# One inverse-root chain for the memory's norm and the convolution's layer norm, and the SiLU by token tile

## The chip, the cores and the metric

The kernel runs on one core of a Trainium2 chip. The metric is the device time of one execution in microseconds (us), median of three runs. The engines that matter: TensorE (PE in the profile; its weight loads are PEld) multiplies matrices, VectorE (DVE) and ScalarE (ACT) do elementwise work, GpSimd (POOL) and SyncE (SP) issue transfers. Each engine works through its own queue in the order in which the program wrote it.

## The reference

Two blocks of a transformer-like model on 256 tokens of width 1024, in float32: retention, MoBA attention and a squared-ReLU MLP in the first; in the second four mixing branches with gates, cross attention to a memory of 256 tokens, and a gated feed-forward part. The change touches the second block's mixing stage and the memory's norm:

```python
c_a, c_g = jnp.split(c_u + b_glu[l], 2, axis=-1)
yc = _dwconv_causal(c_a * jax.nn.sigmoid(c_g), conv_dw[l]) + conv_dw_b[l]     # 31 taps, 512 channels
yc = jax.nn.silu(_layer_norm(yc, conv_ln_g[l], conv_ln_b[l]))
...
br = jnp.stack([ya, yf, yc, ys], axis=2)
proj = jnp.einsum('bsnc,ncd->bsnd', br, w_branch[l])
gates = jax.nn.sigmoid(h @ w_gate[l] + b_gate[l]).reshape(B, S, N_BRANCH, D)
mixed = jnp.sum(gates * proj, axis=2) @ w_out[l]
...
m = _rms_norm(mem, norm_mem[l])                  # x * rsqrt(mean(x * x) + 1e-6) * g
xk, xv = jnp.split(m @ w_xkv[l], 2, axis=-1)
```

Both norms need one inverse square root per token, of a variance for the convolution and of a mean square for the memory.

## The kernel before

Every float32 matrix product is made of three matmuls of rounded parts (`mm3`, L254 to L256): a value is split into a high part, written by ScalarE (`whi`, `brh`, `mth`: L174, L250), and a low part, the difference, written by VectorE (`wlo`, `brl`, `mtl`: L180, L251). Weights come in by SyncE's transfers in chunks of 128x1024 (`raw`), are split so, and used once.

The mixing stage goes through `MIX_STEPS`: eight gate groups (1024 input columns, so two chunks of twelve 128x512 matmuls for each of two token tiles, into `ps_as`) and eight branch groups (twelve matmuls for each token tile, into `ps_br`), first gates 0 and 1, then branch j and gate j+2 in turn up to branch 5, with gates 6 and 7 last and branches 6 and 7 behind them. Branches 6 and 7 are the convolution's (`brh[2]`, `brl[2]`); they are the only consumers of the convolution. All of these outputs, and those of the transposes, go through one pool of four PSUM banks (`bank`), taken in rotation: a group of matmuls can start only when VectorE or ScalarE has read what stood in its bank four allocations earlier. A gate tile is read by VectorE (L1299, the bias), a branch tile by L1316 or by L1318 and L1319 (the gate, then the sum into `part`). When both halves of a `part` are complete, four transposes (`ps_mx`) and a split make the input of the output projection `mix`.

Everything beside the matmuls is threaded between them by `tick`, which runs once behind each group of twelve matmuls: it prepares one or two chunks of weights (two only if no lane is alive and three or more chunks wait), takes one step of every lane (a generator in `lanes` or `light`), then some taps of the convolution from `slow` (L956, VectorE, one 128x256 operation each), then the low parts of the weights. How many taps depends on the same count of lanes: up to three without a lane, otherwise no more than `state["taps"]`.

Three of the lanes matter here. `conv_lane` starts behind branch 4, waits until the taps are done and runs `conv_norm`: transposes `ps_ct` (token tiles to partitions), layer-norm statistics, the inverse root by `rstd` (eleven small VectorE operations on 128x2: a first guess by integer arithmetic and three refinements), `cxn` (L974), two empty steps, transposes back (`ps_ct2`, shown as `ps_ct` in the profile), eight SiLU on ScalarE and the split into `brh`, `brl`. `mem_norm` starts behind branch 3: four squares with row sums on ScalarE (`sqm`, `memss`), an add and its own `rstd` on VectorE, four scalings (L1355), and four groups of four transposes (`pt`, `to_T`) with their splits `mth`, `mtl`, which cross attention reads after the mixing stage. The third is each gate's sigmoid, by `later`.

Of the kernel before, what the change touches and what calls it, by code (L numbers as in the profile page):

```python
# [11 lines left out]
F32 = mybir.dt.float32  # L12
# [87 lines left out]
def tile_model(ctx: ExitStack, tc: tile.TileContext, order, wall, x, mem, gains, gain0, pparam, rparam, w_fg,  # L100
# [17 lines left out]
    def stat(name, w=8, dt=F32):  # L118
        return sp.tile([128, w], dt, tag="st", name=name, bufs=16)
# [202 lines left out]
    def tok(t):  # L322
        return slice(t * 128, t * 128 + 128)
# [636 lines left out]
    def conv_norm():  # L960
        ba, pts = stat("ba", 4), []
# [9 lines left out]
        r = rstd(ba[:, 1:4:2], 2, 1.0, "ln")  # L971
# [4 lines left out]
        yield  # L976
        yield
# [7 lines left out]
        for t in range(2):  # L985
            split(brh[2][:, :, tok(t)], brl[2][:, :, tok(t)], tiles(xns[t]))
# [11 lines left out]

    def conv_lane():
        while slow:  # L1000
            yield
        yield from conv_norm()

# [331 lines left out]

    mth, mtl, memn = {}, {}, []

    def mem_load():
        memn.extend(b4([128, D], f"mem{t}") for t in range(2))
        for t in range(2):  # L1340
            nc.gpsimd.dma_start(memn[t], mem[0, tok(t), :])
        return gain("norm_mem_2")

    def mem_norm(gm):
        ss = stat("memss", 4)
        for t in range(2):
            for n in range(2):
                nc.scalar.activation(t2("sqm"), memn[t][:, HS[n]], AF.Square, accum_out=ss[:, 2 * n + t:2 * n + t + 1])
            yield
        nc.vector.tensor_tensor(ss[:, 0:2], ss[:, 0:2], ss[:, 2:4], op=ALU.add)  # L1350
        r = rstd(ss[:, 0:2], 2, 1.0 / D, "mem")
        yield
        for t in range(2):
            for n in range(2):
                nc.vector.scalar_tensor_tensor(memn[t][:, HS[n]], memn[t][:, HS[n]], r[:, t:t + 1], gm[:, HS[n]],  # L1355
                                               op0=ALU.mult, op1=ALU.mult)
            yield
        yield
        for q in range(2):
            mth[q] = b4([128, 4, 256], f"mth{q}", F32R)  # L1360
            mtl[q] = b4([128, 4, 256], f"mtl{q}", F32R)
        for t in range(2):
            for q in range(2):
                to_T(memn[t], t, mth, mtl, (q,))
                yield

    for kind, j in MIX_STEPS:
# [4 lines left out]
        else:  # L1372
# [6 lines left out]
            if j == 0:  # L1379
                gm = mem_load()  # L1380
            if j == 3:
                ml = lane(mem_norm(gm))
    drain(ml)
# [335 lines left out]
```

## Time and profile before

| | us |
|---|---|
| median of three runs | 1256.43 |
| lowest and highest of the three | 1253.81, 1257.52 |
| profiled execution, own time | 1254.88 |
| its span in the trace | 1253.0 |
| TensorE busy | 1236.9 (99%) |
| VectorE busy | 887.8 (71%) |
| ScalarE busy | 674.0 (54%) |

Times in the trace are counted from the start of the span. The stage that the change touches lies between about 915 and 990. A row's time is that of one instruction from start to end; on TensorE the ends of pipelined matmuls overlap the next start, so that there the distance between two starts is what one costs.

### The profile page before, as it was taken

To read this page: it belongs to the slowest core of one execution; us is meant where nothing else is said; L and a number is where in the kernel's file an instruction comes from. 1 tells how busy PE (TensorE), PEld (TensorE's weight loads), DVE (VectorE), ACT (ScalarE), POOL (GpSimd) and SP (SyncE) were. 2 spreads that over 40 slices of the span, in tenths; PEclk is the share of its full clock that TensorE was granted. 3 is DMA by queue.
4 is the path that set the end of the run, shared out by engine and by line. 5 is a ranking of instruction groups with operands and counts; after the bars stand their busy time and mean duration, and the time that the engine had idled before them with its cause. 6 is when DMAs were issued, how large, how long until landed. Compare 5 with 4: busy or idle time off the path is not lost.

```text
span 1253.0 us, 19058 instructions
## 1 busy us (share of the span) xinstructions
PE 1236.9 (99%) x7352; PEld 1093.7 (87%) x7352; DVE 887.8 (71%) x1570; ACT 674.0 (54%) x1078; POOL 13.0 (1%) x34
## 2 busy tenths in 40 slices
PE   9999999999999999999999999999989999999997
PEld 7888888899988888899988999998877897899996
DVE  7866678755556867765556677878997777588773
ACT  7545355644444765654454546654446466667552
POOL 0000000000000000000000000000000000000000
PEclk9999999999999999999999999999999999999999
DMA  9664473756564545565564644356654554456530
GB/s 366 247 204 152 144 252 135 248 191 192 179 198 159 186 139 171 185 215 189 187 214 156 220 140 143 119 167 215 207 202 168 177 197 164 170 184 192 181 116 35
DMA packets 64924, 228.94 MB, mean 183 GB/s; under 512 B 8256, under 2 KB 8512, under 8 KB 64832
## 3 DMA queue, kind: packets, MB, share of 16 engines
q1 hardware_dynamic: 61808, 217.22, 52.1%
q0 software_dynamic: 2880, 10.49, 2.5%
q8 instruction: 58, 0.95, 0.3%
q14 instruction: 34, 0.28, 0.1%
q10 hardware_dynamic: 144, 0.00, 0.0%
HBM read 226.64 MB, written 1.05 MB: 182 GB/s over the span
## 4 chain that ended last, share of the span: by engine, by line
PE 93%; DVE 3%; ACT 2%; issue 1%; DMA 0%; SPq 0%; DVEq 0%; ACTq 0%
PE ps_ws L254 11%; PE ps_ws L256 11%; PE ps_ws L255 11%; PE ps_as L254 8%; PE ps_as L256 8%; PE ps_as L255 8%; PE mlp L291 4%; PE mlp L290 4%; PE mlp L294 4%; PE ffn L291 1%; PE ffn L290 1%; PE ffn L294 1%; DVE wlo L180 1%; PE ret L290 1%; PE ret L291 1%; PE ret L294 1%
## 5 line engine op out<-in xcount | busy, mean ns | idle before, releaser
L180 DVE TENSOR_TENSOR wlo<-raw,whi 128x1024 fp32r<-128x1024 f32 x404 | 477.6, 1220 | 61.7 <-ACT whi L174 60.7
L174 ACT ACTIVATE whi<-raw 128x1024 fp32r<-128x1024 f32 x404 | 406.6, 1049 | 81.2 <-DVE wlo L180 16.4
L254 PE MATMUL ps_ws<-xhi,whi 128*128 128x256 f32 x1120 | 318.8, 285 | 0.0
L256 PE MATMUL ps_ws<-xhi,wlo 128*128 128x256 f32 x1120 | 316.9, 283 | 0.0
L255 PE MATMUL ps_ws<-xlo,whi 128*128 128x256 f32 x1120 | 316.8, 283 | 0.0
L254 PEld LDWEIGHTS ps_ws<-xhi,whi 128*128 128x128 f32 x1120 | 214.7, 192 | 3.5 <-issue 2.0
L255 PEld LDWEIGHTS ps_ws<-xlo,whi 128*128 128x128 f32 x1120 | 214.8, 192 | 1.5
L256 PEld LDWEIGHTS ps_ws<-xhi,wlo 128*128 128x128 f32 x1120 | 214.7, 192 | 0.0
L254 PE MATMUL ps_as<-whi,xhi 128*128 128x512 f32 x480 | 193.0, 402 | 2.5 <-DVE gates L1318 2.3
L255 PE MATMUL ps_as<-wlo,xhi 128*128 128x512 f32 x480 | 188.2, 392 | 0.4 <-DVE wlo L180 0.4
L256 PE MATMUL ps_as<-whi,xlo 128*128 128x512 f32 x480 | 188.3, 392 | 0.0
L254 PEld LDWEIGHTS ps_as<-whi,xhi 128*128 128x128 f32 x480 | 90.6, 189 | 20.7 <-ACT whi L174 2.5
L256 PEld LDWEIGHTS ps_as<-whi,xlo 128*128 128x128 f32 x480 | 90.5, 189 | 20.4 <-DVE xlo L636 0.4
L255 PEld LDWEIGHTS ps_as<-wlo,xhi 128*128 128x128 f32 x480 | 90.6, 189 | 19.3 <-DVE wlo L180 0.9
L291 PE MATMUL mlp<-wlo,act 128*128 128x512 f32 x240 | 93.7, 390 | 0.0
L290 PE MATMUL mlp<-whi,act 128*128 128x512 f32 x240 | 93.5, 390 | 0.0
L753 DVE SCALAR_TENSOR_TENSOR relu<-ps_ws,relu 128x512 f32<-128x512 f32 x24 | 16.6, 691 | 87.1 <-ACT relu L752 87.1
L752 ACT ACTIVATE relu<-ps_ws 128x512 f32<-128x512 f32 x24 | 14.4, 598 | 113.8 <-PE ps_ws L256 113.8
L294 PE MATMUL mlp<-whi,act 128*128 128x512 f32 x240 | 74.0, 389 | 0.0
L294 PEld LDWEIGHTS mlp<-whi,act 128*128 128x128 f32 x240 | 45.1, 188 | 9.6
L291 PEld LDWEIGHTS mlp<-wlo,act 128*128 128x128 f32 x240 | 45.2, 188 | 8.6
L290 PEld LDWEIGHTS mlp<-whi,act 128*128 128x128 f32 x240 | 45.2, 188 | 8.5
(434 smaller groups left out, 1580.2 us busy)
## 6 DMA issues: line engine op xcount, KB each, us to landing
raw<-in_wall_dram SPq DMA_DIRECT2D x404, 512.0 KB, 4.3
gate_bias<-in_gains_dram POOLq DMA_DIRECT2D x4, 512.0 KB, 5.9
h<-in_x_dram SPq DMA_DIRECT2D x4, 256.0 KB, 5.1
raw<-in_wall_dram SPq DMA_DIRECT2D x4, 256.0 KB, 4.1
gainln_mix_post<-in_gains_dram POOLq DMA_DIRECT2D x2, 512.0 KB, 6.2
gainln_mlp_pre<-in_gains_dram POOLq DMA_DIRECT2D x2, 512.0 KB, 7.8
gainln_mlp_post<-in_gains_dram POOLq DMA_DIRECT2D x2, 512.0 KB, 6.8
mem<-in_mem_dram POOLq DMA_DIRECT2D x2, 512.0 KB, 6.4
```

The source lines that it names most:

```text
L174: nc.scalar.activation(hi, raw, AF.Copy)
L180: nc.vector.tensor_tensor(lo, raw, hi.bitcast(F32), op=ALU.subtract)
L254: nc.tensor.matmul(o, ah, bh, start=start, stop=False)
L255: nc.tensor.matmul(o, ah, bl, start=False, stop=False)
L256: nc.tensor.matmul(o, al, bh, start=False, stop=stop)
L290: nc.tensor.matmul(acc[t][n], ah[:, k, ts], wh[k][:, ns], start=st, stop=False)
L291: nc.tensor.matmul(acc[t][n], ah[:, k, ts], wl[k][:, ns], start=False, stop=False)
L294: nc.tensor.matmul(acc[t][n], al[:, k, ts], wh[k][:, ns], start=False, stop=False)
L752: nc.scalar.activation(r, ps, AF.Relu)
L753: nc.vector.scalar_tensor_tensor(r, ps, 0.0, r, op0=ALU.max, op1=ALU.mult)
```

## The change

The memory's lane is gone. `mem_load` is as before; the four squares now open `conv_lane` (behind branch 4, with the division by 1024 in their scale), the add of the two row sums writes into two further columns of the layer norm's statistics, and one `rstd` over four columns serves both norms. The two empty steps of `conv_norm` now hold the four scalings, one token tile a step. The transposes and splits of the memory became `mem_T`, a lane that starts when `conv_norm` has ended. In `conv_norm` the SiLU and the split go by token tile: four SiLU, split, four SiLU, split.

```diff
     def conv_norm():
-        ba, pts = stat("ba", 4), []
+        ba, pts = stat("ba", 8), []
...
-        r = rstd(ba[:, 1:4:2], 2, 1.0, "ln")
+        nc.vector.tensor_tensor(ba[:, 5:8:2], mss[:, 0:2], mss[:, 2:4], op=ALU.add)
+        r = rstd(ba[:, 1:8:2], 4, 1.0, "ln")
         xns = [t2("cxn") for _ in range(2)]
...
         yield
-        yield
-        yield
+        for t in range(2):
+            for n in range(2):
+                nc.vector.scalar_tensor_tensor(memn[t][:, HS[n]], memn[t][:, HS[n]], r[:, 2 + t:3 + t], memg[0][:, HS[n]],
+                                               op0=ALU.mult, op1=ALU.mult)
+            yield
         br(2)
...
         for t in range(2):
             for i in range(4):
                 nc.scalar.activation(xns[t][:, tok(i)], pts[t][:, tok(i)], AF.Silu, bias=ppc("ln_b", i), scale=ppc("ln_g", i))
-        for t in range(2):
             split(brh[2][:, :, tok(t)], brl[2][:, :, tok(t)], tiles(xns[t]))
         yield
...
+    def mem_T():
+        for q in range(2):
+            mth[q] = b4([128, 4, 256], f"mth{q}", F32R)
+            mtl[q] = b4([128, 4, 256], f"mtl{q}", F32R)
+        for t in range(2):
+            for q in range(2):
+                to_T(memn[t], t, mth, mtl, (q,))
+                yield
+
     def conv_lane():
+        for t in range(2):
+            for n in range(2):
+                nc.scalar.activation(t2("sqm"), memn[t][:, HS[n]], AF.Square, scale=1.0 / math.sqrt(D),
+                                     accum_out=mss[:, 2 * n + t:2 * n + t + 1])
+            yield
         while slow:
             yield
         yield from conv_norm()
+        memg.append(lane(mem_T()))
...
-    def mem_norm(gm):
...
             if j == 4:
                 cl = lane(conv_lane())
             if j == 0:
-                gm = mem_load()
-            if j == 3:
-                ml = lane(mem_norm(gm))
-    drain(ml)
+                mem_load()
+    drain(memg[1])
```

Two consequences can't be seen in the diff. Between branch 3 and branch 4 no lane is alive any more, so `tick` takes more taps and chunks there, and the taps end one tick earlier; with them `conv_norm` starts one tick earlier. The lines of the program shift too: L1299, L1318, L1319, L1355 and L974 of before are L1328, L1347, L1348, L980 and L976 after.

The first place is VectorE around the end of gate 5 and branch 4. Before (the first row is the last of the memory's inverse root; `yc` are taps, `wlo` weights, `gates<-ps_as` and `gates<-ps_br` the reading of a PSUM bank):

```order
L311 SCALAR_TENSOR_TENSOR z_mem<-a_mem,z_mem 128x2
L956 SCALAR_TENSOR_TENSOR yc<-cu,pp,yc 128x232
L956 SCALAR_TENSOR_TENSOR yc<-cu,pp,yc 128x231
L180 TENSOR_TENSOR wlo<-raw,whi 128x1024
L1299 TENSOR_TENSOR gates<-ps_as,gate_bias 128x512
L1355 SCALAR_TENSOR_TENSOR mem_8569<-mem_8569,z_mem,gainnorm_mem_8573 128x512 x2
L956 SCALAR_TENSOR_TENSOR yc<-cu,pp,yc 128x231
L956 SCALAR_TENSOR_TENSOR yc<-cu,pp,yc 128x230
L180 TENSOR_TENSOR wlo<-raw,whi 128x1024
L1318 TENSOR_TENSOR gates<-ps_br,gates 128x512
L1319 TENSOR_TENSOR part<-part,gates 128x512
L1355 SCALAR_TENSOR_TENSOR mem_8570<-mem_8570,z_mem,gainnorm_mem_8573 128x512 x2
```

And after, at the same place of the program:

```order
L956 SCALAR_TENSOR_TENSOR yc<-cu,pp,yc 128x233 x2
L180 TENSOR_TENSOR wlo<-raw,whi 128x1024
L1328 TENSOR_TENSOR gates<-ps_as,gate_bias 128x512
L956 SCALAR_TENSOR_TENSOR yc<-cu,pp,yc 128x232 x2
L956 SCALAR_TENSOR_TENSOR yc<-cu,pp,yc 128x231 x2
L956 SCALAR_TENSOR_TENSOR yc<-cu,pp,yc 128x230 x2
L180 TENSOR_TENSOR wlo<-raw,whi 128x1024
L1328 TENSOR_TENSOR gates<-ps_as,gate_bias 128x512
L956 SCALAR_TENSOR_TENSOR yc<-cu,pp,yc 128x229 x2
L180 TENSOR_TENSOR wlo<-raw,whi 128x1024 x2
L1347 TENSOR_TENSOR gates<-ps_br,gates 128x512
L1348 TENSOR_TENSOR part<-part,gates 128x512
```

The memory's chain and its four scalings have left, and taps that stood later have come in front of branch 4.

The second place is VectorE from the end of the layer norm's inverse root to branch 6. Before:

```order
L311 SCALAR_TENSOR_TENSOR z_ln<-a_ln,z_ln 128x2
L974 TENSOR_SCALAR cxn<-ps_ct,ba,z_ln 128x512 x2
L180 TENSOR_TENSOR wlo<-raw,whi 128x1024
L1299 TENSOR_TENSOR gates<-ps_as,gate_bias 128x512
L180 TENSOR_TENSOR wlo<-raw,whi 128x1024 x2
L1299 TENSOR_TENSOR gates<-ps_as,gate_bias 128x512
L251 TENSOR_TENSOR brl_9416<-cxn,brh_9415 128x4x128 x2
L180 TENSOR_TENSOR wlo<-raw,whi 128x1024 x2
L1318 TENSOR_TENSOR gates<-ps_br,gates 128x512
L1319 TENSOR_TENSOR part<-part,gates 128x512
```

And after:

```order
L311 SCALAR_TENSOR_TENSOR z_ln<-a_ln,z_ln 128x4
L976 TENSOR_SCALAR cxn<-ps_ct,ba,z_ln 128x512 x2
L180 TENSOR_TENSOR wlo<-raw,whi 128x1024
L980 SCALAR_TENSOR_TENSOR mem_8570<-mem_8570,z_ln,gainnorm_mem_8574 128x512 x2
L180 TENSOR_TENSOR wlo<-raw,whi 128x1024
L1328 TENSOR_TENSOR gates<-ps_as,gate_bias 128x512
L980 SCALAR_TENSOR_TENSOR mem_8571<-mem_8571,z_ln,gainnorm_mem_8574 128x512 x2
L180 TENSOR_TENSOR wlo<-raw,whi 128x1024
L251 TENSOR_TENSOR brl_9345<-cxn,brh_9344 128x4x128 x2
L180 TENSOR_TENSOR wlo<-raw,whi 128x1024
L1328 TENSOR_TENSOR gates<-ps_as,gate_bias 128x512
L180 TENSOR_TENSOR wlo<-raw,whi 128x1024
```

The two pairs of memory scalings now stand between `cxn` and the split `brl` of the convolution, each with a chunk of weights behind it.

The third is TensorE around the transposes of the convolution's normed tiles. Before, at the end of gate 7 and the start of branch 6 (the numbers are those of the tiles):

```order
L254 MATMUL ps_as_9379<-whi_9155,xhi_6474 128x512
L255 MATMUL ps_as_9379<-wlo_9156,xhi_6474 128x512
L256 MATMUL ps_as_9379<-whi_9155,xlo_6476 128x512
L317 MATMUL ps_ct2_9417<-ident_98,cxn_9352 128x128 x4
L317 MATMUL ps_ct2_9418<-ident_98,cxn_9353 128x128 x4
L254 MATMUL ps_br_9449<-whi_9188,brh2_9415 128x512
L255 MATMUL ps_br_9449<-wlo_9189,brh2_9415 128x512
L256 MATMUL ps_br_9449<-whi_9188,brl2_9416 128x512
```

And after, where these are rows from the middle of gate 7's second token tile:

```order
L254 MATMUL ps_as_9328<-whi_9061,xhi_6473 128x512
L255 MATMUL ps_as_9328<-wlo_9062,xhi_6473 128x512
L256 MATMUL ps_as_9328<-whi_9061,xlo_6475 128x512
L317 MATMUL ps_ct2_9346<-ident_98,cxn_9277 128x128 x4
L317 MATMUL ps_ct2_9347<-ident_98,cxn_9278 128x128 x4
L254 MATMUL ps_as_9328<-whi_9087,xhi_6474 128x512
L255 MATMUL ps_as_9328<-wlo_9088,xhi_6474 128x512
L256 MATMUL ps_as_9328<-whi_9087,xlo_6476 128x512
```

The transposes now have the last twelve matmuls of gate 7 behind them and branch 6 only after those. The four groups of transposes of the memory, which stood in branch 5 and gate 6, now stand in branches 6 and 7, one behind each twelve matmuls; on ScalarE the rows `cxn` (SiLU) and `brh` alternate as the diff shows.

## Rows read from the trace of the kernel before

**Rows 1.** Page, busy time and share of the span of each engine.
```profile
PE 1236.9 (99%) x7352; PEld 1093.7 (87%) x7352; DVE 887.8 (71%) x1570; ACT 674.0 (54%) x1078; POOL 13.0 (1%) x34
```

**Rows 2.** What TensorE waited for, whole span: us, times, longest.
```profile
PE ps_br L254 <- ACT brh L250: 3.1, 1, 3.1
PE ps_as L254 <- DVE gates L1318: 2.3, 1, 2.3
```

**Rows 3.** Windows: busy (x) of PE, PEld, DVE, ACT, POOL; clock, DMA share, GB/s.
```profile
920.00:930.00 10.00, 9.91 (x46) 7.87 (x44) 9.90 (x18) 4.79 (x7) 0.00 (x0) 1.00 0.60 193
930.00:940.00 10.00, 6.84 (x26) 5.42 (x27) 9.89 (x16) 3.46 (x5) 0.00 (x0) 0.83 0.43 147
...
960.00:970.00 10.00, 6.92 (x23) 5.08 (x22) 5.59 (x8) 9.45 (x16) 0.00 (x0) 0.83 0.46 159
```

**Rows 4.** PE's timeline at the second place: start, us, instruction, idle before.
```profile
956.44 0.39 PE L254 MATMUL ps_as<-whi,xhi 128*128 128x512 f32 x1
...
959.16 1.03 PE L317 MATMUL ps_ct<-ident,cxn 128*128 128x128 f32 x8
963.27 0.50 PE L254 MATMUL ps_br<-whi,brh 128*128 128x512 f32 x1 [3.08 <-ACT brh L250]
...
964.81 0.59 PE L256 MATMUL ps_br<-whi,brl 128*128 128x512 f32 x1
...
968.18 0.43 PE L255 MATMUL ps_br<-wlo,brh 128*128 128x512 f32 x1
```

**Rows 5.** PE's timeline at the first place.
```profile
929.53 0.39 PE L256 MATMUL ps_br<-whi,brl 128*128 128x512 f32 x1
930.89 0.66 PE L317 MATMUL pt<-ident,mem 128*128 128x128 f32 x4 [0.98 <-DVE gates L1318]
933.82 0.50 PE L254 MATMUL ps_as<-whi,xhi 128*128 128x512 f32 x1 [2.27 <-DVE gates L1318]
934.12 0.62 PE L255 MATMUL ps_as<-wlo,xhi 128*128 128x512 f32 x1
...
937.53 0.40 PE L254 MATMUL ps_as<-whi,xhi 128*128 128x512 f32 x1
```

**Rows 6.** DVE's timeline at the first place.
```profile
918.08 0.15 DVE L1350 TENSOR_TENSOR memss<-memss 128x2 f32<-128x2 f32 x1
...
920.33 0.82 DVE L956 SCALAR_TENSOR_TENSOR yc<-cu,pp,yc 128x232 f32<-128x232 f32 x2
...
922.80 1.40 DVE L1355 SCALAR_TENSOR_TENSOR mem<-mem,z_mem,gainnorm_mem 128x512 f32<-128x512 f32 x2
924.13 0.82 DVE L956 SCALAR_TENSOR_TENSOR yc<-cu,pp,yc 128x231 f32<-128x231 f32 x2
...
932.99 0.68 DVE L1318 TENSOR_TENSOR gates<-ps_br,gates 128x512 f32<-128x512 f32 x1
...
934.31 0.69 DVE L251 TENSOR_TENSOR mtl<-pt,mth 128x512 fp32r<-128x512 f32 x1
```

**Rows 7.** ACT's timeline at the second place.
```profile
958.13 1.28 ACT L984 ACT_TABLE_LOAD   x1
959.80 2.90 ACT L984 ACTIVATE cxn<-ps_ct,pp 128x128 f32<-128x128 f32 x8 [0.39 <-PE ps_ct L317]
962.56 1.18 ACT L250 ACTIVATE brh<-cxn 128x512 fp32r<-128x512 f32 x2
```

**Rows 8.** DVE's timeline ahead of the second place.
```profile
947.58 0.69 DVE L1299 TENSOR_TENSOR gates<-ps_as,gate_bias 128x512 f32<-128x512 f32 x1 [0.62 <-PE ps_as L256]
...
949.32 0.69 DVE L969 BATCH_NORM_STATS2 bs<-ps_ct 128x6 f32<-128x512 f32 x1
...
953.23 1.53 DVE L974 TENSOR_SCALAR cxn<-ps_ct,ba,z_ln 128x512 f32<-128x512 f32 x2
954.68 1.21 DVE L180 TENSOR_TENSOR wlo<-raw,whi 128x1024 fp32r<-128x1024 f32 x1
955.81 0.68 DVE L1299 TENSOR_TENSOR gates<-ps_as,gate_bias 128x512 f32<-128x512 f32 x1
```

More of the change, by code (lines that the diff above doesn't have):

```diff
@@ L997, in tile_model, with mem_load @@
         ws_chunk(("list256", "w_in_2", C_U + i * 128, C_U + 512 + i * 128), evac)
-    def conv_lane():
+    mth, mtl, memn, memg = {}, {}, [], []
+    mss = cp.tile([128, 4], F32, name="memss")
+    def mem_load():
+        memn.extend(b4([128, D], f"mem{t}") for t in range(2))
+        for t in range(2):
+            nc.gpsimd.dma_start(memn[t], mem[0, tok(t), :])
+        memg.append(gain("norm_mem_2"))
+    def mem_T():
[6 more added lines that the diff above has]
+                yield
+    def conv_lane():
+        for t in range(2):
+            for n in range(2):
+                nc.scalar.activation(t2("sqm"), memn[t][:, HS[n]], AF.Square, scale=1.0 / math.sqrt(D),
+                                     accum_out=mss[:, 2 * n + t:2 * n + t + 1])
+            yield
         while slow:
@@ L1333, in mixed @@
             split(a[0][:, :, tok(t)], a[1][:, :, tok(t)], tiles(pt[:, c * 256:c * 256 + 256]))
[L1336 to L1342, printed above, removed]
-    def mem_norm(gm):
[L1345 to L1365, printed above, removed]
     for kind, j in MIX_STEPS:
```

## The prediction

> **What bounds the kernel now.** I read the page's busy times first, then what TensorE waited for, then the ten-microsecond windows of the changed stretch, and last the timelines of TensorE, VectorE and ScalarE there. The busy times [rows 1] name TensorE: 1236.9 of 1253.0 us, with VectorE at 71% and ScalarE at 54%. So an instruction taken off VectorE or ScalarE is worth only the wait of TensorE that it ends. The two longest of those waits [rows 2] stand in the stage that the change touches: 3.1 us for `brh` on ScalarE and 2.3 us for an evacuation on VectorE (L1318). The windows [rows 3] show what else they cost: 930 to 940 and 960 to 970 have TensorE busy for 6.84 and 6.92 us, and the granted clock, 1.00 in the window before, is 0.83 in both.
>
> **The price of the two places.** TensorE's steady pitch is 2.72 us for twelve 128x512 matmuls (956.44 to 959.16 [rows 4]), 0.227 us each.
> First place: the `pt` transposes at 930.89 waited 0.98 us and the first matmul of gate 6, at 933.82, waited 2.27 us [rows 5]: 3.25 us. Then the matmuls run at the lower of the clock's two levels (1.2 GHz): eight from 934.12 to 937.53 take 3.41 us where 1.82 would do, 1.59 lost, and the first pitch (0.30) loses 0.07. Sum 4.91.
> Second place: branch 6 at 963.27 waited 3.08 us [rows 4]; its first five pitches, to 964.81, take 1.54 instead of 1.14 (0.40 lost), the next eight, to 968.18, 3.37 instead of 1.82 (1.55 lost). Sum 5.03.
> Together 9.94 us. This is the most that this stage can give.
>
> **Part 1, VectorE around branch 4.** Before, VectorE stands some 6 us behind TensorE there: the evacuation for which gate 6 waits starts at 932.99 [rows 6] and belongs to the first unit of branch 5, which ended before the second unit's 2.72 us began, and that one's last matmul stands at 929.53 [rows 5], so around 927. What put it behind is in the same rows: the chain of small `memss`/`z_mem` operations from 918.08 to 920.33 (2.25 us for twelve, 0.19 each) and the two pairs of memory scalings (922.80 to 924.13, so 1.33 a pair, 2.66 together). Further on, four `mtl` splits (0.69 at 934.31, of which the next operation overlaps 0.08, as everywhere on this engine: 0.6) stand among the evacuations of branch 5 and gate 6. All of that leaves. In exchange four more taps come ahead of branch 4 (0.82 a pair at 920.33, so 0.74), which is work that stood a little later, not new work. So VectorE reaches the first evacuation of branch 4 about when its matmuls end, and the distance of 6 us shrinks to one or two. The waits of 0.98 and 2.27 us need a lag of more than the three spare banks; I take both, and the slow clock behind them, as gone: -4.91.
> The four groups of transposes that leave this place are not saved, they stand later on TensorE: 0. The four squares on ScalarE, each about as long as a `brh` (1.18 for two [rows 7]), now start a little later in a stretch where ScalarE is idle more than half of the time (4.79 us busy from 920 to 930 [rows 3]): 0.
>
> **Part 2, from the layer norm to branch 6.** The transposes `ps_ct2` now stand ahead of the last twelve matmuls of gate 7, so ScalarE has 2.72 us of TensorE's work as a cover that it did not have. Before, the SiLU started 0.64 us after the transposes (959.16 [rows 4], 959.80 [rows 7]), eight took 2.90 us with the splits right behind at 962.56 (0.35 each to there), and TensorE stood until 963.27. After, counted from the end of gate 6 as zero: TensorE runs gate 7 (48 matmuls, 10.88) with the eight transposes in it (1.03 in their row [rows 4], which the next matmul overlaps by some 0.2, so 0.8), so branch 6 could start at 11.7 and its third matmul, the first that reads `brl`, at 12.15.
> ScalarE: the transposes start at 8.16, SiLU of tile 0 at 8.8, four SiLU end at 10.2, the split at 10.8. `brh` is 0.9 us early. The table load of 1.28 us stands ahead of it with nothing queued before it that is late: hidden, with over a microsecond to spare. Were the cover gone, its 1.28 us would lie on the path.
> VectorE: already before, it waited 0.62 us for the end of this gate tile (947.58 [rows 8]); with less ahead of it, it waits longer. Then it has, in one queue: the evacuation (0.2 until it starts, for a matmul's row ends 0.16 after its pitch; 0.69 less 0.08, 0.60); the statistics and the inverse root, 3.91 (949.32 to 953.23 [rows 8]), plus one small add, 0.19; `cxn` 1.45; weights 1.13 (954.68 to 955.81); memory tile 0, 1.33; weights 1.13; evacuation 0.60; memory tile 1, 1.33; weights 1.13. That is 13.0. The inverse root over four columns instead of two I take at the same price, since 512 columns cost 0.60 us and 2 columns 0.19, so that two more add nothing that shows. Then `brl` of tile 0, the shape of `mtl`, 0.65: ready at 13.65. **TensorE is there at 12.15, so the third matmul of branch 6 waits 1.5 us.** This is a new wait: the memory scalings and a weight split, not the SiLU, now stand ahead of `brl`. Queued behind that matmul is all of TensorE. The bounds are 0 (VectorE 1.5 us ahead of this walk) and the 3.08 of before.
> So of 5.03 us this part returns about 3.5: -3.5.
>
> **Part 3, branches 6 and 7.** The transposes of the memory now stand between their units. A unit of TensorE is 2.72 plus four transposes, some 0.4: 3.1 us. VectorE has per unit two operations of the evacuation (932.99 to 934.31 [rows 6], 1.32), `mtl` 0.6 and weights 1.13: 3.06. They are level, and four banks lie between them. In the last two units a pair of `act` splits comes on top; I expect up to 0.2 us, and take 0. Its upper bound is the first place of before, where the same mixture made TensorE wait 3.25 us.
>
> **Sum.** -4.91 - 3.5 = -8.4 us. Against the profiled execution's own 1254.88 us that is 1246.5; the median of the three runs stands 1.55 us above that execution, so on the median 1256.43 I forecast **1248.0 us**. The runs of before lie 3.7 us apart; 0.3% (3.8 us) is about what a measurement here can tell from no change.
>
> **The rivals.**
> *The clock falls after the new wait.* Both places of before were followed by the lower level, and what 0.98 us does by itself can't be told, because 2.27 us come right behind it. If 1.5 us is enough, 1.6 to 2.0 us come back: 1249.8. The Trainium skill, "TensorE: Matmul & The Clock Gate", section "HAM oscillation — how this bites in real kernels", has a kernel whose every wait between groups of matmuls is followed by a group at half clock; the trace agrees for 2.27 and 3.08 us, and no run here shows 1.5. Chance 0.25.
> *No new wait.* VectorE keeps up and the whole 9.9 us are gained: 1246.5 on the median. Against it: the sum of 13.65 has no large uncertain term. Chance 0.12.
> *The second place is only renamed.* If `brl` or `brh` comes 3 us late after all, only the first place pays, -4.9: 1251.5. For it: some twenty operations of VectorE between gate 6 and `brl` have to follow one another without a hole. Chance 0.09.
> *Nothing moves.* If TensorE's busy rows were not what sets the time, the two waits would be filled elsewhere: 1256.4. The Trainium skill, "Perfetto Trace Analysis", section "Identifying the Most-Contended Engine", holds the busy share of matmuls a poor measure, and wants the share of weight loads read instead; by that 87% [rows 1] would leave 13% open on TensorE. Against the mechanism: while nothing is waited for, the matmuls keep 0.227 us apart, and the share not busy in the two windows is what the two waits add up to. The same end results if new waits of 6 us or more in branches 6 and 7 eat the gain. Chance 0.07.
> *Slower.* One mechanism: VectorE's queue in branches 6 and 7. If each of the four units with memory transposes costs what the first place cost with its clock, 4.91, that is +19.6 - 8.4, or 1267.6. One such unit leaves a gain of 3.5; two make it slower by 1.4; it takes two and a half to be slower by over 0.3%. For it: the same operations did stop TensorE before. Against it: they met VectorE then with 6 us of lag and taps in the queue, and there are no taps left here. Chance 0.04.
>
> **How the numbers follow.** The forecast itself has 0.43. Its own range, from 0.7 us more or less of the new wait and the scatter of the runs, is 1246.5 to 1249.5. Forecast, clock fall, no wait and part of the third rival make 0.8 with 1245.0 to 1251.3. Faster by over 0.3% (below 1252.7): 0.43 + 0.25 + 0.12 + 0.09, less a little for the scatter, 0.88. Within 0.3%: 0.08. Slower: 0.04.
>
> **What would show it.** Right: no wait for L1318 around branch 5, clock 1.00 there; VectorE idle for a microsecond or two before the last evacuation of gate 6; `ps_ct2` followed by twelve gate matmuls; one wait of some 1.5 us at the third matmul of branch 6, put down to `brl`, none to `brh`; no wait above 0.3 us among the memory's transposes. Wrong: a wait on `pt` or `ps_mx` in branches 6 and 7, a wait on `brh`, or a clock below 1.00 around branch 6.

## The result, and the profile after

| | before, us | after, us |
|---|---|---|
| median of four runs | 1256.76 | 1245.97 |
| lowest and highest | 1253.81, 1257.52 | 1245.57, 1246.07 |
| profiled execution, own time | 1254.88 | 1246.03 |
| its span | 1253.0 | 1244.3 |

Of before, a fourth run (1257.09) has joined the three that the forecast started from. The ratio of the means is 0.9918, with a 95% interval of 0.9901 to 0.9935: faster by 0.8%. The forecast was 1248.0 with a range of 1245.0 to 1251.3. Against the profiled executions the sum of the prediction, -8.4 us, meets -8.85; the medians lie 10.8 us apart, for a reason that the last section takes up.

The page's first line, and the list of what TensorE waited for (us in total, times, longest), both of the changed kernel:

```profile
PE 1233.0 (99%) x7352; PEld 1091.8 (88%) x7352; DVE 885.7 (71%) x1559; ACT 674.0 (54%) x1078; POOL 13.0 (1%) x34
```

```profile
PE warm L621 <- POOL ident masks.py:199: 1.4, 1, 1.4
PE ps_br L256 <- DVE brl L251: 1.2, 1, 1.2
```

The two waits of [rows 2] are gone from the list. In their place stands one of 1.2 us, for `brl`. TensorE's busy time fell by 3.9 us with the same 7352 matmuls, about the 3.6 us that the prediction gave the slow clock. The windows of the stage (columns as in [rows 3]) say the same:

```profile
930.00:940.00 10.00, 10.00 (x50) 8.37 (x49) 9.64 (x14) 5.46 (x9) 0.00 (x0) 1.00 0.69 227
...
950.00:960.00 10.00, 8.77 (x44) 7.01 (x43) 9.90 (x14) 9.65 (x17) 0.00 (x0) 1.00 0.63 211
```

Where 930 to 940 had 6.84 us of TensorE at a clock of 0.83 there are now 10.00 at 1.00, and the only window that is not full, 950 to 960, lacks 1.23 us.

The timelines around the second place, first VectorE's:

```profile
930.37 0.69 DVE L1347 TENSOR_TENSOR gates<-ps_br,gates 128x512 f32<-128x512 f32 x1
...
941.65 0.69 DVE L1328 TENSOR_TENSOR gates<-ps_as,gate_bias 128x512 f32<-128x512 f32 x1 [1.94 <-PE ps_as L256]
...
946.23 1.53 DVE L976 TENSOR_SCALAR cxn<-ps_ct,ba,z_ln 128x512 f32<-128x512 f32 x2
...
948.81 1.41 DVE L980 SCALAR_TENSOR_TENSOR mem<-mem,z_ln,gainnorm_mem 128x512 f32<-128x512 f32 x2
...
951.87 1.41 DVE L980 SCALAR_TENSOR_TENSOR mem<-mem,z_ln,gainnorm_mem 128x512 f32<-128x512 f32 x2
...
954.33 1.29 DVE L251 TENSOR_TENSOR brl<-cxn,brh 128x512 fp32r<-128x512 f32 x2
```

then ScalarE's:

```profile
947.12 1.28 ACT L989 ACT_TABLE_LOAD   x1 [2.21 <-DVE cxn L976]
950.25 1.51 ACT L989 ACTIVATE cxn<-ps_ct,pp 128x128 f32<-128x128 f32 x4 [1.85 <-PE ps_ct L317]
951.79 0.63 ACT L250 ACTIVATE brh<-cxn 128x512 fp32r<-128x512 f32 x1
```

then TensorE's:

```profile
949.62 1.03 PE L317 MATMUL ps_ct<-ident,cxn 128*128 128x128 f32 x8
...
953.23 0.39 PE L254 MATMUL ps_br<-whi,brh 128*128 128x512 f32 x1
953.45 0.39 PE L255 MATMUL ps_br<-wlo,brh 128*128 128x512 f32 x1
955.07 0.50 PE L256 MATMUL ps_br<-whi,brl 128*128 128x512 f32 x1 [1.23 <-DVE brl L251]
955.40 0.40 PE L254 MATMUL ps_br<-whi,brh 128*128 128x512 f32 x1
```

Read them against the walk of the prediction. VectorE waits 1.94 us for the end of gate 6 (941.65), and from there it has no hole until `brl` begins at 954.33. `brh` of tile 0 was ready at 952.42 (951.79 and 0.63), 0.8 us before branch 6 could start; TensorE issued that branch's first two matmuls at 953.23 and 953.45, stood 1.23 us, and took the third at 955.07. The next one followed after 0.33 us and from there on all were at the full clock. The memory's transposes, between the units of branches 6 and 7, have no entry in the list of waits.

### The profile page after: what moved, and what is told of

The parts are those of the page before. It is cut to its first block, busy times and chain, and to the rows that moved or that the text cites. A ratio compares the mean times of both kernels' runs of the same rounds, so it can differ in the third digit from the quotient of the medians.

```text
span 1244.3 us, 19056 instructions
## 1 busy us (share of the span) xinstructions
PE 1233.0 (99%) x7352; PEld 1091.8 (88%) x7352; DVE 885.7 (71%) x1559; ACT 674.0 (54%) x1078; POOL 13.0 (1%) x34
## 4 chain that ended last, share of the span: by engine, by line
PE 94%; DVE 3%; ACT 2%; issue 1%; DMA 0%; SPq 0%; DVEq 0%; ACTq 0%
PE ps_ws L254 11%; PE ps_ws L255 11%; PE ps_ws L256 11%; PE ps_as L256 8%; PE ps_as L254 8%; PE ps_as L255 8%; PE mlp L291 4%; PE mlp L290 4%; PE mlp L294 4%; PE ffn L291 1%; PE ffn L290 1%; PE ffn L294 1%; PE ps_br L256 1%; PE ps_br L255 1%; PE ps_br L254 1%; DVE wlo L180 1%
```

## The experiments

All of them ran beside the kernel before; a median is that of four runs unless it says otherwise, and of ten for two of them.

**1. What the SiLU by token tile is worth.** The changed kernel with whole SiLU:

```diff
             for i in range(4):
                 nc.scalar.activation(xns[t][:, tok(i)], pts[t][:, tok(i)], AF.Silu, ...)
+        for t in range(2):
             split(brh[2][:, :, tok(t)], brl[2][:, :, tok(t)], tiles(xns[t]))
```

> The changed kernel, with the eight SiLU first and then both splits, as before. My theory: the SiLU by token tile is not what pays, since the split of tile 0 (brl on VectorE) waits for VectorE's queue and not for ScalarE. In the changed kernel brh of tile 0 was ready at 952.4 and brl began at 954.33; with whole SiLU brh comes some 1.5 us later, 953.9, still ahead of 954.33. TensorE would then wait some 0.7 us for brh (953.23 to 953.9) and 0.8 instead of 1.23 us for brl: the same time as the changed kernel, 1246.0, within 0.5 us. Rival, the SiLU by tile is what ended the second wait: 1.5 us or more come back, 1247.5 to 1249, with the longest wait put down to brh.

Measured 1246.10 us, ratio 0.9923 (0.9906 to 0.9939): the changed kernel's time. Its waits:

```profile
PE ps_br L256 <- DVE brl L251: 0.6, 1, 0.6
...
PE ps_br L254 <- ACT brh L250: 0.3, 1, 0.3
```

The time is the one forecast. The 1.2 us for `brl` split up into 0.3 for `brh` and 0.6 for `brl`, where 0.7 and 0.8 were reckoned: the waits were over-sized, but counted between the starts of the matmuls the two together cost the same 1.4 us as the one wait did. So in the changed kernel this part of the edit is hidden behind VectorE.

**2. The same part alone, on the kernel before.** The reverse of that diff.

> The kernel before with the SiLU and the split by token tile and nothing else. My theory: without a cover the SiLU is on the path there, so parting it pays where it stands: brh of tile 0 comes 1.4 us earlier, the wait at branch 6 falls from 3.08 to 1.7 us, and brl of tile 0 right behind, so that a second wait of 0.2 to 0.3 us comes at the third matmul. Gain 1.1 to 1.4 us, and 2.7 to 3.2 if the clock then stays up: 1253.5 to 1255.3 against 1256.6. Rival, brl or the table load decides and nothing is gained: 1256.6.

Measured 1252.70 us (ten runs, 1251.75 to 1255.43) against 1255.35 of before (nineteen runs), ratio 0.9983 (0.9973 to 0.9993). So without a cover it does pay. How much of the 2.65 us is its own can't be read from the medians, because of the clock: three of the ten runs have a mean granted clock of 0.995, the others 0.998 to 0.999, and in the trace the clock differs already at the first place, ahead of the edit. TensorE's timeline at the first place:

```profile
931.77 0.66 PE L317 MATMUL pt<-ident,mem 128*128 128x128 f32 x4 [0.97 <-DVE gates L1317]
934.68 0.47 PE L254 MATMUL ps_as<-whi,xhi 128*128 128x512 f32 x1 [2.26 <-DVE gates L1317]
934.99 0.39 PE L255 MATMUL ps_as<-wlo,xhi 128*128 128x512 f32 x1
935.22 0.40 PE L256 MATMUL ps_as<-whi,xlo 128*128 128x512 f32 x1
```

This is the wait of [rows 5], 0.97 and 2.26 us, and behind it the matmuls stand 0.23 us apart, not 0.43. At the second place `brh` was waited for 2.29 us, more than the 1.7 that I gave. With no slow matmuls ahead, TensorE was there 0.7 us earlier, and the SiLU could not follow, since it began as soon as its table was loaded (958.29 and 1.28, then 959.58). ScalarE's rows, then TensorE's wait:

```profile
958.29 1.28 ACT L984 ACT_TABLE_LOAD   x1
959.58 1.50 ACT L984 ACTIVATE cxn<-ps_ct,pp 128x128 f32<-128x128 f32 x4
961.12 0.63 ACT L250 ACTIVATE brh<-cxn 128x512 fp32r<-128x512 f32 x1
...
961.80 0.50 PE L254 MATMUL ps_br<-whi,brh 128*128 128x512 f32 x1 [2.29 <-ACT brh L250]
```

**3. What the shared chain is worth.** The changed kernel with a chain of its own for the memory, at the same place:

```diff
-        nc.vector.tensor_tensor(ba[:, 5:8:2], mss[:, 0:2], mss[:, 2:4], op=ALU.add)
-        r = rstd(ba[:, 1:8:2], 4, 1.0, "ln")
+        nc.vector.tensor_tensor(mss[:, 0:2], mss[:, 0:2], mss[:, 2:4], op=ALU.add)
+        rm = rstd(mss[:, 0:2], 2, 1.0, "mem")
+        r = rstd(ba[:, 1:4:2], 2, 1.0, "ln")
...
```

> The changed kernel, with an inverse-root chain of its own for the memory again, at the place of the shared one. My theory: the stretch from gate 6 to brl is VectorE's, so the eleven small operations come on the path with their full time, some 2.1 us: the wait for brl grows from 1.23 to 3.3 us, and the clock falls behind it as it did before (1.6 to 2.0 us more): 1246.0 + 3.7 to 4.1, so 1249.7 to 1250.1. Rival, the chain is hidden (its sum is ready long before, and a wait on something else ends last): 1246.0, no change in the wait. Second rival, the wait grows but the clock stays: 1248.1.

Measured 1250.17 us, ratio 0.9957 (0.9943 to 0.9972): 4.2 above the changed kernel, where 3.7 to 4.1 were forecast. TensorE's timeline:

```profile
954.09 0.47 PE L254 MATMUL ps_br<-whi,brh 128*128 128x512 f32 x1 [0.74 <-ACT cxn L990]
...
957.06 0.73 PE L256 MATMUL ps_br<-whi,brl 128*128 128x512 f32 x1 [2.27 <-DVE brl L251]
957.59 0.63 PE L254 MATMUL ps_br<-whi,brh 128*128 128x512 f32 x1
958.02 0.63 PE L255 MATMUL ps_br<-wlo,brh 128*128 128x512 f32 x1
```

Waits of 0.74 and 2.27 us in place of 1.23, and behind them a pitch of 0.43. The profile puts the 0.74 down to a SiLU of the second token tile, which this unit does not read. VectorE's reading of gate 7's first tile, whose bank the unit takes, ended just then too (953.26 and 0.68 us, where it begins at 951.27 in the changed kernel); which of the two was waited for is not shown. Eleven operations of 0.2 us cost four microseconds at this place, 1.7 of them by the clock (eight pitches from 957.06 to 960.58 take 3.52 us, not 1.82).

**4. The same chain at another place.** The kernel before, with the start of the memory's lane moved and everything else as it was:

```diff
-            if j == 3:
+            if j == 5:
                 ml = lane(mem_norm(gm))
```

> The kernel before, with one line changed: the memory's lane starts behind branch 5 and not behind branch 3. Its chain of its own stays, and the SiLU stays whole. My theory: the place of the memory's work is what pays, not the sharing of the chain. The chain falls where VectorE waits for gate 6 in any case (1.94 us idle in the changed kernel), the taps move as in the changed kernel, the transposes back get their cover, and the scalings stand ahead of brl as there. Expected: first place gone, one wait of 1.2 to 2 us at branch 6, 1246.0 to 1246.8, the time of the changed kernel within 0.8 us. Rival, the sharing is what pays: some 2.2 us of chain come back on the path, 1248.2 or more.

Measured 1249.21 us (1247.83 to 1249.58), ratio 0.9949 (0.9933 to 0.9966): my number was missed by 2.4 to 3.2. The profiled execution is the fastest of the four (1247.83, granted clock 0.999 on the mean of the whole execution); the other three, 1249.15 to 1249.58, have a mean of 0.997, so a stretch at the lower clock fits for them, on top of what the trace shows. What it shows is neither the chain nor `brl`:

```profile
953.59 0.66 PE L317 MATMUL pt<-ident,mem 128*128 128x128 f32 x4 [2.81 <-DVE gates L1299]
```

In this order the first memory transposes stand in gate 7, and their bank is the one of gate 7's first tile, which VectorE reads only behind both memory scalings. So a further empty step ahead of the transposes was put in, which brings them behind gate 7 and between the units:

```diff
             yield
         yield
+        yield
         for q in range(2):
             mth[q] = b4([128, 4, 256], f"mth{q}", F32R)
```

> The kernel before with the memory's lane started behind branch 5 and one more empty step ahead of its transposes, so that these stand behind branch 6's units as in the changed kernel; the chain of its own and the whole SiLU stay. In the run with the lane behind branch 5 alone, the longest wait was 2.8 us of the first memory transposes for a PSUM bank (they had moved into gate 7), and none was left for brh or brl; its own chain ended with VectorE only 0.3 us later at the layer norm than in the changed kernel. My theory: what made that run slower is the bank, not the chain. Expected here: the waits of the run with whole SiLU (0.3 for brh, 0.6 to 0.9 for brl), 1246.0 to 1246.6. Rival, the chain costs its 2.2 us: 1248.0 or more, with a wait of 3 us for brl.

Measured 1248.31 us (1247.61 to 1248.48), ratio 0.9938 (0.9923 to 0.9954). By the number alone the rival, 1248.0 or more, would have it; its wait of 3 us for `brl` is not there (0.6). VectorE's timeline further on, first of the changed kernel and then of this one:

```profile
993.58 0.68 DVE L385 TENSOR_TENSOR y<-mix,gainnorm_mix_post 128x512 f32<-128x512 f32 x1
...
1052.16 1.42 DVE L411 SCALAR_TENSOR_TENSOR h<-y,r,h 128x512 f32<-128x512 f32 x2
```

```profile
993.57 0.68 DVE L385 TENSOR_TENSOR y<-mix,gainnorm_mix_post 128x512 f32<-128x512 f32 x1
...
1052.14 1.42 DVE L411 SCALAR_TENSOR_TENSOR h<-y,r,h 128x512 f32<-128x512 f32 x2
```

At the end of the output projection and again 59 us later the two kernels stand at the same time to 0.02 us. The whole difference between these two executions, 1.6 us (2.3 between the medians), comes behind that, in the first matmuls of the next stage:

```profile
1060.72 0.50 PE L254 MATMUL ps_as<-whi,xhi 128*128 128x512 f32 x1 [0.34 <-ACT whi L174]
1061.98 0.50 PE L255 MATMUL ps_as<-wlo,xhi 128*128 128x512 f32 x1 [0.76 <-DVE wlo L180]
```

These wait for weights (`whi`, `wlo`), which `tick` prepares; that the one tick that this kernel has fewer in the mixing stage makes them late fits (ScalarE has split 51 chunks from 900 to 1055 us and not 52, and is one behind from 980 on), but no run tried it. In the mixing stage itself a chain of its own, put where VectorE waits for gate 6 in any case, costs nothing. Sharing is worth 4 us where the chain stands on the path and, in that stage, nothing where it stands in the hole; why the kernel as a whole is still slower stays open.

**5. What the chain did at the first place.** The kernel before with the memory scaled by its sum of squares, without the inverse root (this part of the norm is left out):

```diff
-        r = rstd(ss[:, 0:2], 2, 1.0 / D, "mem")
+        r = ss
```

> The kernel before without the memory's inverse root (the sum of squares scales the memory instead, so this part of the norm is left out): eleven small operations fewer on VectorE, all else in its place. My theory: the chain is one part of VectorE's lag of 6 us at the first place, so 2.0 us of the waits there end: 0.98 vanishes and 2.27 becomes 1.2 or so, and if the clock then stays up another 1.6 us: second place untouched. Gain 2.0 without, 3.6 with the clock: 1253 to 1254.7 against a median of 1256.6. Rival, the chain alone made the first place: the whole 4.9 us are gained, 1251.7, no wait on L1318 left.

Measured 1252.23 us (ten runs) against 1255.35, ratio 0.9974 (0.9965 to 0.9983). At the first place one wait is left:

```profile
932.99 0.47 PE L254 MATMUL ps_as<-whi,xhi 128*128 128x512 f32 x1 [1.40 <-DVE gates L1318]
```

1.40 us in place of 0.98 and 2.27, so 1.85 us for 2.1 us of VectorE's operations, and the clock stayed up there. The second place did not stay as it was: TensorE was there earlier, the SiLU began only behind its table load (956.59 and 1.28, then 957.88), and the wait for `brh` grew from 3.08 to 3.59 us, with a longer stretch at the lower clock behind it. This profiled execution, 1254.00, is the slowest of the ten. The chain made more than half of the first place's wait; what made the rest, the scalings, the `mtl` splits or their places, no run took apart.

**6. The cover of the SiLU.** The changed kernel with one more step ahead of the transposes back:

```diff
             yield
+        yield
         br(2)
```

> The changed kernel with one more empty step ahead of the transposes back, so that they stand right ahead of branch 6, as before; scalings and SiLU by tile as in the changed kernel. My theory: the twelve gate matmuls behind the transposes are the cover of the SiLU. Without them TensorE stands from the end of the transposes until brh of tile 0 is there: SiLU 0.64 us after the transposes begin, four of them 1.45, split 0.6, that is 2.7 less the 0.8 of the transposes, 1.9 us, and with brl behind it another 0.3 or so: 2.2 to 2.5 us instead of 1.23, and perhaps the lower clock behind it. 1247.0 to 1247.3 without the clock's fall, 1248.6 to 1249.3 with it. Rival, the cover is worth nothing because VectorE's queue decides: 1246.0 within 0.4.

Measured 1250.22 us, ratio 0.9958 (0.9943 to 0.9972). Without the cover the kernel is 4.2 us slower, more than I forecast. ScalarE's timeline has the term that I left out, and the last row is TensorE's wait:

```profile
952.01 0.63 ACT L1330 ACTIVATE gates<-gates 128x512 f32<-128x512 f32 x1 [7.08 <-DVE gates L1329]
...
953.60 1.28 ACT L990 ACT_TABLE_LOAD   x1
954.89 1.50 ACT L990 ACTIVATE cxn<-ps_ct,pp 128x128 f32<-128x128 f32 x4
...
957.11 0.80 PE L254 MATMUL ps_br<-whi,brh 128*128 128x512 f32 x1 [3.71 <-ACT brh L250]
```

The sigmoid of gate 7's first tile (952.01), which in the changed kernel stands behind the SiLU, now stands ahead of it in ScalarE's queue, and had waited 7.08 us for VectorE's evacuation of that tile. Behind it come a chunk of weights and the table load, 1.28 us, and the SiLU starts 0.01 us after that. So the table load was on the path, and TensorE's wait was 3.71 us, not 2.2 to 2.5, with the slow clock behind it (pitches of 0.43). In the changed kernel the same load began at 947.12 and was done 1.85 us before the SiLU could start. The 4.2 us are thus the cover, the order in ScalarE's queue and the clock together.

**7. More work ahead of `brl`.** The changed kernel with two more scalings into a spare tile, read by nobody:

```diff
+        for _ in range(2):
+            nc.vector.scalar_tensor_tensor(t2("dum"), memn[0][:, HS[0]], r[:, 2:3], memg[0][:, HS[0]], op0=ALU.mult, op1=ALU.mult)
         br(2)
```

> The changed kernel with two more 128x512 scalings into a spare tile on VectorE, ahead of brl (1.33 us of work that nothing reads). My theory: brl is set by VectorE's queue, so the wait at the third matmul of branch 6 grows by 1.33, from 1.23 to 2.56 us, and 1.3 us come on the time: 1247.3. As to the clock: before, it fell behind waits of 3.08 and of 0.98 and 2.27 together, and in the changed kernel it stayed at 1.00 behind 1.23. If 2.56 is enough, 1.6 us more: 1248.9. Rival, VectorE's queue has room: 1246.0.

Measured 1249.04 us, ratio 0.9947 (0.9932 to 0.9962).

```profile
956.31 0.80 PE L256 MATMUL ps_br<-whi,brl 128*128 128x512 f32 x1 [2.54 <-DVE brl L251]
956.90 0.63 PE L254 MATMUL ps_br<-whi,brh 128*128 128x512 f32 x1
957.33 0.63 PE L255 MATMUL ps_br<-wlo,brh 128*128 128x512 f32 x1
```

A wait of 2.54 us, 1.31 more than 1.23 for 1.33 us of work, and then the lower clock: both numbers as forecast.

**8. Four ways to take the new wait away.** First, the second memory tile's scaling between the two `brl`:

```diff
-        for t in range(2):
+        def scale_mem(t):
             for n in range(2):
...
-            yield
+        scale_mem(0)
+        yield
+        yield
         br(2)
...
             split(brh[2][:, :, tok(t)], brl[2][:, :, tok(t)], tiles(xns[t]))
+            if t == 0:
+                scale_mem(1)
         yield
```

> The changed kernel, with the scalings of the memory's second token tile between the brl splits of tile 0 and tile 1 and no longer ahead of both. My theory: brl of tile 0 then starts 1.33 us earlier, 953.0, just where TensorE needs it (953.68), and the last new wait ends: 1.2 to 1.5 us less, 1244.6. VectorE's work in branches 6 and 7 is the same in the same order, so nothing is late behind it; a wait of up to 0.5 us on pt or ps_br would show that I am wrong there. Rival, something beside the scalings holds brl (brh on ScalarE, weights): 1246.0 and the wait still there.

Measured 1246.01 us, ratio 0.9923 (0.9908 to 0.9938). The wait for `brl` is gone and the time is the same. Here I was wrong: work behind it was late enough to take the gain back.

```profile
968.30 0.63 PE L317 MATMUL ps_mx<-ident,part 128*128 128x128 f32 x4 [0.46 <-DVE act L251]
```

The last `ps_mx` transposes wait 0.46 us for an `act` split, and with smaller delays ahead of them the first `mix` matmul starts at 968.68, 0.04 us from where it starts in the changed kernel (968.72). That made VectorE's queue as a whole the suspect, and two kernels take the scalings off it. In both, ScalarE multiplies by the inverse root ahead of its table load. The gain is multiplied by GpSimd behind the squares in the one, and by VectorE in its hole of 1.94 us in the other:

```diff
+                nc.gpsimd.tensor_tensor(memn[t][:, HS[n]], memn[t][:, HS[n]], memg[0][:, HS[n]], op=ALU.mult)    # the one
...
+                nc.vector.tensor_tensor(memn[t][:, HS[n]], memn[t][:, HS[n]], memg[0][:, HS[n]], op=ALU.mult)    # the other, ahead of the statistics
...
-                nc.vector.scalar_tensor_tensor(memn[t][:, HS[n]], memn[t][:, HS[n]], r[:, 2 + t:3 + t], memg[0][:, HS[n]], ...)
+                nc.scalar.activation(memn[t][:, HS[n]], memn[t][:, HS[n]], AF.Copy, scale=r[:, 2 + t:3 + t])
```

> The changed kernel with the memory's scaling taken off VectorE: GpSimd multiplies by the gain right behind the squares, and ScalarE by the inverse root ahead of its table load, where it stands idle. When the wait for brl alone was taken away (memory tile 1 between the two brl), the whole gain came back as lateness of the ps_mx splits on VectorE, so that my theory now is: from the end of gate 6 to the first mix matmuls VectorE's queue as a whole is the bound. Without its 2.66 us of scalings brl starts when brh is there (952.4), ahead of TensorE (953.7), and the splits for mix are early too: 1.4 us less than the changed kernel, 1244.6. Rival, another bound stands right behind (ScalarE's SiLU, a bank): 1245.5 to 1246. A GpSimd that slows VectorE's operations while it works would show in their durations around 930.

Measured 1248.98 us, ratio 0.9944 (0.9929 to 0.9960): slower than the changed kernel by 3.0. GpSimd's four multiplications (930.11 to 937.65), VectorE's timeline while they run, and last a tap of the changed kernel, where GpSimd stands still:

```profile
930.11 7.54 POOL L1027 TENSOR_TENSOR mem<-mem,gainnorm_mem 128x512 f32<-128x512 f32 x4 [29.49 <-ACT sqm L1025]
...
931.07 0.69 DVE L1348 TENSOR_TENSOR gates<-ps_br,gates 128x512 f32<-128x512 f32 x1
931.79 1.07 DVE L1349 TENSOR_TENSOR part<-part,gates 128x512 f32<-128x512 f32 x1
932.78 1.49 DVE L956 SCALAR_TENSOR_TENSOR yc<-cu,pp,yc 128x227 f32<-128x227 f32 x1
934.19 2.30 DVE L180 TENSOR_TENSOR wlo<-raw,whi 128x1024 fp32r<-128x1024 f32 x1
```

```profile
931.70 0.45 DVE L956 SCALAR_TENSOR_TENSOR yc<-cu,pp,yc 128x227 f32<-128x227 f32 x1
```

A tap takes 1.49 us and not 0.45, a weight split 2.30 and not 1.22, an add of two SBUF tiles 1.07 and not 0.69; the evacuation L1348, with one operand in PSUM, takes 0.68 to 0.69 as ever. The taps are late by that, and TensorE waits 1.21 us for the last of them. At the first `mix` matmul (970.79) the kernel is 2.1 us behind the changed one, 0.7 of which stood there already ahead of the edit; the rest of the 3.0 us comes later and was not followed.

> The same, with the gain's four multiplications on VectorE, but in the hole of 1.94 us in which it waits for the end of gate 6 in the changed kernel; ScalarE multiplies by the inverse root. VectorE then has 2.66 us less between the layer norm and branch 6, and reaches the last evacuation of gate 6 some 0.4 us later than before. Same theory: no wait for brl, 1244.6 to 1245.0. Rival, the hole is too short and the taps or the weights behind it make TensorE wait: a wait on wlo or ps_ct around 942 and 1245.5 or more.

Measured 1246.23 us, ratio 0.9923 (0.9905 to 0.9941): no gain, with the scalings out of the way. VectorE's timeline:

```profile
952.74 0.69 DVE L251 TENSOR_TENSOR brl<-cxn,brh 128x512 fp32r<-128x512 f32 x1 [0.54 <-ACT brh L250]
954.80 0.69 DVE L251 TENSOR_TENSOR brl<-cxn,brh 128x512 fp32r<-128x512 f32 x1 [1.37 <-ACT brh L250]
...
957.69 1.23 DVE L180 TENSOR_TENSOR wlo<-raw,whi 128x1024 fp32r<-128x1024 f32 x1 [0.47 <-ACT whi L174]
```

Now it stands 0.54 and 1.37 us before the two `brl`, waiting for `brh`, and 0.47 us for weights that ScalarE splits behind its second table load. So its evacuation of branch 6's first unit comes at 958.84, 0.28 us later than in the changed kernel (958.56), and TensorE waits again for an `mtl` split and for `ps_mx` (0.5 each). Part of that is the edit's own: ScalarE's four scalings (2.57 us from 946.67) put its table load at 949.24, and the SiLU began right behind the load, at 950.54, 0.29 us later than in the changed kernel. Without that shift the evacuation would come about where it comes in the changed kernel, by this estimate no sooner. So ScalarE's chain of SiLU, splits and table loads stands right behind VectorE's queue as the next bound; a run with ScalarE unburdened too was not made.

Last, the kernel of the first way with the memory's transposes two steps later, so that one of their four groups goes into the output projection and two `mtl` splits fewer stand ahead of the `act` splits:

```diff
     def mem_T():
...
+        for _ in range(2):
+            yield
         for t in range(2):
             for q in range(2):
                 to_T(memn[t], t, mth, mtl, (q,))
...
-    drain(memg[1])
+    tick()
```

> The kernel with memory tile 1 scaled between the two brl, and the memory's transposes started two steps later, so that two of their four groups stand in branch 6 and 7, one behind them and one inside the output projection. Where that kernel took the wait for brl away, 0.8 us of it came back at the last ps_mx transposes, which waited for VectorE (act splits behind three mtl splits). My theory, VectorE's queue from gate 6 to the first mix matmuls is the bound: with two mtl splits of 0.6 us fewer ahead of those act splits, the 0.8 us stay gained: 1245.2 to 1245.6. Rival, the time is held by ScalarE's SiLU and its table loads or by the four banks, which the kernel with the gain in VectorE's hole pointed to (2.3 us less on VectorE and no gain): 1246.0, with the wait moved to another transpose.

Measured 1247.15 us (five runs), ratio 0.9924 (0.9911 to 0.9938, against a before of 1256.67 beside it): a miss on the slow side, 1.2 above the changed kernel, which ran beside another measurement of before. Half a microsecond of that stands already ahead of the edit (the first memory scaling begins at 949.32, not at 948.81) and is not its work. The rest is a wait that moved to the banks:

```profile
967.30 0.63 PE L317 MATMUL pt<-ident,mem 128*128 128x128 f32 x4 [0.55 <-PE ps_mx L317]
968.99 0.66 PE L317 MATMUL ps_mx<-ident,part 128*128 128x128 f32 x4 [1.06 <-DVE gates L1355]
```

The last transposes need the bank of branch 7's last unit, whose evacuation VectorE starts at 968.25. No version here beats the changed kernel.

## Why the prediction was right, point by point

**The first place, -4.91.** Right: no wait for L1318 (now L1347) is left and the clock is 1.00. One statement on the way to it was mis-sized. VectorE's distance did not shrink from 6 us to one or two: it starts the evacuation of branch 5's first unit at 930.37, some 3.4 us after that unit's end. That is inside what four banks bear, so that the conclusion stood on the banks and not on that size. In experiment 5 the chain made 1.85 of the 3.25 us; experiment 4 shows that moving the lane alone ends all of it.

**The second place, -3.5.** The walk held: VectorE's hole 1.94 us (one or two forecast), `brl` of tile 0 ready 13.6 us after the end of gate 6 (13.65), TensorE at its third matmul 12.2 (12.15), `brh` 0.8 us early (0.9), and a wait of 1.23 us, 1.4 between the starts, where 1.5 was forecast. The chain over four columns cost what it had cost over two (3.97 us from the statistics to `cxn` with the add, 4.10 forecast). Experiments 3 and 7 show that the length of VectorE's queue sets it, almost microsecond for microsecond, experiment 6 that the cover does the rest, with the table load that was counted as hidden and would else be on the path.

**Branches 6 and 7, 0.** Right as measured, but closer to the edge than I had it: the term "up to 0.2, and take 0" holds only while TensorE comes late. Experiment 8 shows that 1.2 us less of waiting ahead of them comes back as waits in them and right behind them. So the rival "no new wait", 1246.5, could not have been had by VectorE keeping up at `brl` alone.

**The rivals.** By its number alone the median, 1245.97, would belong to "no new wait" (1246.5), and it lies below the forecast's own range of 1246.5 to 1249.5; only the wait of 1.23 us for `brl`, where the walk had put it, tells the forecast from that rival. The clock did not fall behind 1.23 us. It fell behind 2.54 us in experiment 7 and behind 2.27 in experiment 3, so that the rival was one microsecond away. "Nothing moves" fell with the two waits. The Trainium skill, "Perfetto Trace Analysis", section "Identifying the Most-Contended Engine", would have TensorE's headroom judged by the share of peak throughput that it reaches and by its weight loads. The weight loads were at 87% and are at 88%, while the gain lay in two waits that no busy share shows; the list of waits was the view that priced it.

**The sum.** Two profiled executions differ by 8.85 us (forecast 8.4). The 1.55 us between the profiled execution of before and its median were added on both sides, and that is the term that was mis-sized; with the 0.45 above it makes the 2.0 by which the forecast of the median was too high. The changed kernel's runs lie within 0.5 us of each other, and its profiled execution at the median, so there was nothing to add. That the changed median still fell inside the wide range of 1245.0 to 1251.3 is owed to the rival "no new wait", which that range took in.

## What to carry to other kernels

Price an operation by the queue that it stands in: eleven operations of 0.2 us cost 4 us ahead of a split that TensorE waits for (with the slow clock that followed), 1.85 us of waiting where they add to a lag, and nothing in a hole. When one wait is taken away, look for what stands level behind it before counting the gain; here VectorE's queue, ScalarE's chain and the four banks all end within a microsecond of each other. Give a chain that changes engines (transposes, table load, SiLU, split) some matmuls of cover, and look at what is queued ahead of its table load.

## What the runs showed of the hardware that was not expected

**The same wait is not always followed by the slow clock.** Behind 0.98 and 2.27 us the matmuls stood 0.43 us apart in the kernel before [rows 5], and 0.23 apart behind 0.97 and 2.26 in experiment 2. Behind 2.81 us (experiment 4's first kernel) the window's clock was 1.00, behind 2.29 us (experiment 2, second place) it fell. A stretch at the lower level cost 1.4 to 1.7 us in the traces [rows 4, 5], and 2.9 us behind the 3.59 us of experiment 5 (fourteen pitches from 961.35 to 967.40 take 6.05 us, not 3.18). This fits with how the kernel before, with two such places, scatters over 4 us (nineteen runs from 1253.76 to 1257.91, in which I see groups around 1254.1, 1255.4 and 1257.2), and the changed one over 0.5. The mean granted clock of each execution goes with the groups: 0.997 to 0.998 in the first, 0.996 to 0.997 in the second and 0.994 to 0.995 in the third, with 0.998 to 0.999 in the changed kernel. So the slower executions of before did spend more time at the lower level, and the 1.55 us by which the median of before stands above its profiled execution fit there, though the clock of those runs is not on record. That the groups are one, two or three stretches is an argument from their distance of 1.3 to 1.8 us and from these means; where a third stretch would stand no trace shows. The Trainium skill, "TensorE: Matmul & The Clock Gate", section "HAM oscillation — how this bites in real kernels", has a kernel in which every wait between its groups of matmuls, some 3 to 5 us by its figure, brings a cold group; the runs here, with mostly shorter waits, agree for most waits above 2 us and not for all.

**GpSimd slows VectorE.** While it multiplied 128x512 tiles (7.54 us for four), VectorE's operations with two inputs in SBUF took 1.6 to 3.3 times as long, and those with one in PSUM did not change (experiment 8). What the two engines contend for was not tried.
